# Mixer outputs normed with tokens in the rows, RWKV values centred on the way, and one of ten plans followed

## The chip, the cores and the metric

The kernel runs on one core of a Trainium2 chip. The metric is the device time of one execution in microseconds (us), the median of several runs. All data are float32. The core has a matrix engine (PE in the profile, with its weight loads shown as PEld), a vector engine (DVE), a scalar engine (ACT), GpSimd (POOL) and an engine that issues the DMAs (SP). Each follows its own instruction list in order and waits on semaphores for the others.

## The reference

Two layers of a streaming encoder over 1024 tokens of width 1024. Each layer is: RMS norm, one wide input projection, two mixers side by side, one output projection, RMS norm and residual add, and then a gated MLP of width 2816 with norm and residual. Layer 0 mixes with RWKV-7 (8 heads of 64) and a spatial gating unit; layer 1 with HGRN2 (8 heads of 64) and gated DeltaNet (4 heads of 128). The change touches only what happens to a mixer's output `y`, per token and head:

```python
# RWKV-7: layer norm over a head's 64 values, bonus, gate
mu_y = jnp.mean(y, axis=-1, keepdims=True)
var_y = jnp.mean(jnp.square(y - mu_y), axis=-1, keepdims=True)
y = ((y - mu_y) * lax.rsqrt(var_y + RWKV_LN_EPS) * ln_g + ln_b)
y = y + jnp.sum(rh * kh * r_k, axis=-1, keepdims=True) * vh
y = y * g
# HGRN2: RMS norm over a head's 64 values, then the gate
return merge_heads(rms_norm(o, norm_g)) * silu(gate)
# gated DeltaNet: RMS norm over a head's 128 values, then the gate
return merge_heads(rms_norm(o, norm_g)) * silu(z)
```

In RWKV-7 the state is linear in the values `v`, and so is `y`: if every `v` has its mean over the head's 64 channels taken away, so has `y`.

## The kernel before

**Two kinds of work share PE.** The projections and the MLP are dense matmuls (`dense`): weights come in pieces of 256 KB, ACT makes a rounded copy `wh` of each and DVE the remainder `wl`, and three matmuls `d<-h,wh`, `d<-l,wh`, `d<-h,wl` of 128 x 512 replace each float32 product (`mh`, `ml` in place of `h`, `l` in the second half of the MLP). The mixers are cut into units of 256 tokens and 128 channels: 16 RWKV units (`rwkv_unit`), 16 HGRN2 units (`hgrn_unit`) and 16 DeltaNet units (`gdn_unit`), each a chain of small float32 matmuls into PSUM banks called `m`, with short DVE, ACT and POOL steps between them. A unit has channels in the partitions and tokens in the columns; tokens come in 4 chunks of 64.

**A unit's tail before.** The products of all chunks are added up in one bank `py`, channels in the rows. RWKV copies it out (`yy`, on ACT), multiplies by the centring matrix `cen` on PE, squares on ACT (`sq`) and copies the centred values on DVE (`yc`). Then `rsqrt` sums the squares per head by a matmul with columns of ones (`m<-blk,sq`, or `m<-ones,sq` for DeltaNet), scales on DVE and takes the power -1/2 on POOL (`rt`), spreads the result over each head's 64 columns on ACT (`rw`; DeltaNet reads `rt` itself with a repeated column), and turns it on PE (`m<-ident,rw`, `m<-ident,rt`), so that two DVE steps can multiply by norm and weight. HGRN2 and DeltaNet do the same without the centring. RWKV ends with a gate matmul (`m<-L,gup`). Each result goes to DRAM by a DMA.

**The order is planned.** `Plan` records the whole program twice. The first pass only counts buffers; the second places every instruction by costs of its own on a clock of its own, always resuming the most urgent thread that can go (mixer units before the MLP). Where a unit reaches a `yield` with a list of tiles, it is not resumed until `MARGIN` (1.0 us on the plan's clock) after these are ready, and other threads fill PE until then. The order found is then fixed on each engine. At most 4 units are open at a time, and the input projection runs at most 1 unit group ahead.

Every instruction is issued from one helper line, L66, so tiles tell the profile's rows apart, not lines.

Of the kernel before, what the change touches and what calls it, by code (L numbers as in the profile page):

```python
# [23 lines left out]
C = 64  # L24
# [51 lines left out]
PACE = 0.8  # L76

MARGIN = 1.0
# [32 lines left out]
class Plan:  # L111
# [4 lines left out]
    def __init__(self, nc, past=None, tc=None):  # L116
        self.nc, self.past, self.tc = nc, past, tc
        names = ("tensor", "vector", "scalar", "gpsimd", "sync")
# [144 lines left out]
    def place(self, eng, method, outs, ins, scaled=False, func=None):  # L263
# [71 lines left out]
        t += c  # L335
        if eng == "tensor":
# [68 lines left out]
    def run(self, threads, queue, limit):  # L405


        units = 0
        self.live = live = list(threads)
        while live:  # L410
# [5 lines left out]
            if self.past:  # L416
                w = int(self.now // TICK)
                if self.work.get(w, 0.0) < PACE * 3060 * (self.now / TICK - w):
                    todo = [(t, u - 10 if x.dense else u, i, x) for t, u, i, x in todo]
# [12 lines left out]
            else:  # L432
                x.wake = max((self.ready.get(ap.tensor.name, (0.0, 0))[0] for ap in need), default=-MARGIN) + MARGIN


class Trunk:
    kp, kahead, over, smooth = 4, 2, 1, 1

    def __init__(self, ctx, tc, a, out, past=True):
        if past is True:  # L440
            past = forecast(a)
        self.h, self.l = ([[None] * 2 for _ in range(KT)] for _ in range(2))
        self.tc, self.nc, self.a, self.out = tc, Plan(tc.nc, past, tc), a, out
# [662 lines left out]


# [59 lines left out]
    def rwkv_unit(self, j, u, NC):  # L1167
# [215 lines left out]
        nc.vector.scalar_tensor_tensor(out=yy, in0=yy, scalar=col["ln_g"], in1=rs, op0=ALU.mult, op1=ALU.mult)  # L1383
        nc.vector.scalar_tensor_tensor(out=yy, in0=yy, scalar=col["ln_b"], in1=bon, op0=ALU.add, op1=ALU.add)
# [110 lines left out]
    def hgrn_unit(self, j, u, NC):  # L1495
# [83 lines left out]
        py = m()  # L1579
# [3 lines left out]
        for n in range(0 if S0 is not None else 1, NC):  # L1583
            for h in range(2):
# [3 lines left out]
        nc.vector.tensor_copy(yy, py[:, 0:W])  # L1588
        sq = t("sq", (P, W))
        nc.scalar.activation(sq, py[:, 0:W], AF.Square)  # L1590
        yield [sq]
        rs = yield from self.rsqrt(sq, 2, 1.0 / 64, 4 * EPS)
        nc.vector.scalar_tensor_tensor(out=yy, in0=yy, scalar=self.col["hhng"][:, j:j + 1], in1=rs, op0=ALU.mult, op1=ALU.mult)
        nc.vector.tensor_tensor(out=yy, in0=yy, in1=gate, op=ALU.mult)
# [104 lines left out]
    def gdn_unit(self, h, u, NC):  # L1699
# [115 lines left out]
        nc.vector.tensor_copy(yy, py[:, 0:W])  # L1815
        sq = t("sq", (P, W))
        nc.scalar.activation(sq, py[:, 0:W], AF.Square)
        yield [sq]
        rs = yield from self.rsqrt(sq, 1, 1.0 / P, EPS)
        nc.vector.scalar_tensor_tensor(out=yy, in0=yy, scalar=self.col["hgng"], in1=rs, op0=ALU.mult, op1=ALU.mult)  # L1820
        nc.vector.tensor_tensor(out=yy, in0=yy, in1=zz, op=ALU.mult)
# [50 lines left out]
    def run(self):  # L1872
# [7 lines left out]
        self.groups, self.workers, self.ahead = [5, 5, 4, 4, 4], 4, 1  # L1880
        self.urg = dict(unit=0, mix=-1, sgu=1, mixers=2, ffn=3, start=1, rows=2.5)
# [20 lines left out]
        self.nc.run(threads, self.units, self.workers)  # L1902
# [51 lines left out]
```

## Time and profile before

| | |
|---|---|
| median of 3 runs | 2949.36 us (2948.76 to 2951.91) |
| the profiled execution's own time | 2953.02 us |
| its span, first to last instruction | 2951.3 us |
| PE busy | 2836.7 us, 96% |
| DVE busy | 1843.5 us, 62% |
| ACT busy | 1258.8 us, 43% |
| POOL busy | 574.9 us, 19% |
| mean granted PE clock | 0.977 |

A matmul's span in these rows is longer than its share of PE, since the next one starts before it ends: 128 x 512 matmuls last some 0.4 us and start every 0.23 us. What one costs PE is read from the distance of starts in the timeline. A float32 matmul of the program shows as two records, a transpose as one, a dense matmul as one. In a timeline row `m<-blk,sq 128*128 128x2 f32 x4` the first product is the stationary operand's rows by columns, then the output's partitions by moving columns, then the number of records that stand one after another. Brackets at a row's end tell how long the engine had been idle, and what ended that.

### The profile page before, as it was taken

The numbers are of one execution on the slowest core, as the hardware profiler recorded it, in microseconds if no ns is written. First come the engines' busy times: TensorE is split into PE (matmuls) and PEld (weight loads), VectorE is DVE, ScalarE is ACT, GpSimd is POOL, SyncE is SP. The second block draws the span as 40 slices with busy tenths as digits, with TensorE's granted clock in tenths as the row PEclk, the third lists the DMA queues.
The fourth block names the chain that finished last, engine by engine and source line by source line (L and its number), as shares of the span: only waits on it lengthen the run. The fifth ranks groups of instructions, "written<-read, shape, count | busy, mean of one in ns | idle before, by whom it ended". The sixth has DMA issues, their size and how long they took to land. (4 is left out here: it accounts for less than half of the span.)

```text
span 2951.3 us, 46440 instructions
## 1 busy us (share of the span) xinstructions
PE 2836.7 (96%) x16608; PEld 2285.5 (77%) x16608; DVE 1843.5 (62%) x3747; ACT 1258.8 (43%) x2435; POOL 574.9 (19%) x1527
## 2 busy tenths in 40 slices
PE   7998999899999999999999999999999999999998
PEld 6776777778878877777778878777777888888886
DVE  4857686785574476666665676657666557554444
ACT  4445363454443355333334344543333335444333
POOL 1345233352000000323440000032343000000000
PEclk9998999899999999999999999999999999999999
DMA  6233244222443344545333444464642344343332
GB/s 178 66 88 83 73 141 129 56 71 80 128 141 91 99 141 86 90 72 68 77 77 114 127 121 125 104 97 60 83 82 62 93 133 134 107 127 88 108 96 93
DMA packets 560228, 294.13 MB, mean 100 GB/s; under 512 B 103293, under 2 KB 533198, under 8 KB 559998
## 3 DMA queue, kind: packets, MB, share of 16 engines
q1 hardware_dynamic: 559998, 291.17, 40.0%
q8 instruction: 131, 2.15, 0.3%
q14 instruction: 99, 0.81, 0.1%
HBM read 255.37 MB, written 35.71 MB: 99 GB/s over the span
## 5 line engine op out<-in xcount | busy, mean ns | idle before, releaser
L66 PE MATMUL d<-h,wh 128*128 128x512 f32 (+1 forms) x2544 | 1045.5, 411 | 0.0
L66 PE MATMUL d<-h,wl 128*128 128x512 f32 (+1 forms) x2544 | 1011.8, 398 | 4.9 <-DVE wl L66 4.9
L66 PE MATMUL d<-l,wh 128*128 128x512 f32 (+1 forms) x2544 | 1011.3, 398 | 0.0
L66 ACT CAST wh<-wr 128x512 fp32r<-128x512 f32 (+1 forms) x860 | 507.6, 594 | 700.7 <-PE d L66 555.2
L66 DVE TENSOR_TENSOR wl<-wr,wh 128x512 fp32r<-128x512 f32 (+1 forms) x860 | 560.4, 664 | 229.7 <-ACT wh L66 223.2
L66 PEld LDWEIGHTS d<-h,wl 128*128 128x128 f32 (+1 forms) x2544 | 482.6, 190 | 122.6 <-DVE wl L66 8.8
L66 PEld LDWEIGHTS d<-h,wh 128*128 128x128 f32 (+1 forms) x2544 | 483.6, 190 | 105.9 <-issue 2.2
L66 PEld LDWEIGHTS d<-l,wh 128*128 128x128 f32 (+1 forms) x2544 | 483.9, 190 | 98.3 <-issue 0.7
L66 POOL TENSOR_TENSOR rt<-rt,mhalf 128x4 f32<-128x4 f32 (+1 forms) x94 | 104.5, 1113 | 964.0 <-DVE rt L66 927.6
L66 PE MATMUL d<-mh,wh 128*128 128x512 f32 x704 | 283.9, 403 | 0.0
L66 PE MATMUL d<-mh,wl 128*128 128x512 f32 x704 | 279.3, 397 | 1.5 <-DVE wl L66 1.5
L66 PE MATMUL d<-ml,wh 128*128 128x512 f32 x704 | 279.1, 396 | 0.0
L66 DVE SCALAR_TENSOR_TENSOR t<-g,col,t 128x512 f32<-128x512 f32 x176 | 133.0, 755 | 168.0 <-ACT t L66 155.4
L66 POOL TENSOR_TENSOR itm<-iN,iPT 32x48 f32<-32x48 f32 (+15 forms) x480 | 160.6, 335 | 172.2 <-DMA iN<-ib 77.5
L66 POOL TENSOR_TENSOR iPT<-iPT,itm 32x48 f32<-32x48 f32 (+15 forms) x480 | 177.9, 371 | 36.2
L66 DVE TENSOR_TENSOR acc<-acc,d 128x512 f32<-128x512 f32 x128 | 88.0, 688 | 125.5 <-PE d L66 125.0
L66 PEld LDWEIGHTS d<-mh,wl 128*128 128x128 f32 x704 | 133.1, 189 | 34.2 <-DVE wl L66 3.2
L66 PEld LDWEIGHTS d<-mh,wh 128*128 128x128 f32 x704 | 133.4, 189 | 30.4 <-issue 0.2
L66 PEld LDWEIGHTS d<-ml,wh 128*128 128x128 f32 x704 | 133.3, 189 | 29.2 <-DVE ml L66 0.3
L66 ACT COPY g<-d 128x512 f32<-128x512 f32 x88 | 51.6, 587 | 149.7 <-PE d L66 149.3
L66 POOL COPY fhalo<-g 128x2 f32<-128x2 f32 x44 | 11.0, 249 | 473.3 <-ACT g L66 473.3
L66 DVE TENSOR_TENSOR sq<-sq 128x512 f32<-128x512 f32 x97 | 67.2, 693 | 23.7 <-ACT sq L66 17.7
(339 smaller groups left out, 3208.6 us busy)
## 6 DMA issues: line engine op xcount, KB each, us to landing
wr<-in_ffn_w_in SPq DMA_DIRECT2D x352, 256.0 KB
wr<-in_od_w_in SPq DMA_DIRECT2D x128, 256.0 KB
wr<-in_ffn_w_out SPq DMA_DIRECT2D x96, 256.0 KB
wr<-in_ev_w_in SPq DMA_DIRECT2D x84, 256.0 KB
xt<-xd SPq DMA_DIRECT2D x56, 256.0 KB
wr<-in_ffn_w_out SPq DMA_DIRECT2D x64, 192.0 KB
wr<-in_ev_w_out SPq DMA_DIRECT2D x32, 256.0 KB
yl<-yd SPq DMA_DIRECT2D x32, 256.0 KB
```

The source lines that it names most:

```text
L66: r = fn(*args, **kw)
```

## The change

**Tails.** In all three units the last products swap their operands, so that tokens stand in the rows of `py` and channels in the columns. A new function `normed_rows` squares on ACT straight from PSUM, sums per head with a DVE reduction, scales on DVE, takes the power on POOL, multiplies out of PSUM on DVE (`yt`), and only then transposes `yt` on PE. The sums by matmul, the spread `rw` and the turning of the norm go. HGRN2 now holds two banks, one per head, and squares and multiplies each by itself. **Centring.** RWKV's values `v` are transposed by a matmul with `cen` in place of the identity, so `y` comes out centred and the product with `cen` at the tail goes. **Plans.** `MARGIN` and other constants become fields of ten rules; each rule's plan is made, and the one whose end on the plan's clock is earliest is followed. For this program it is the second: everything as before, but a margin of 0.7 in place of 1.0.

```diff
-PACE = 0.8
-MARGIN = 1.0
+RULES = [dict(dict(pace=0.8, margin=1.0, workers=4, ahead=1, second=1), **r) for r in (
+    {}, dict(margin=0.7), dict(margin=0.85), dict(margin=1.3), dict(ahead=2), dict(second=-1), dict(workers=5),
+    dict(pace=0.9), dict(margin=0.7, ahead=2), dict(margin=0.85, workers=5))]
...
-                x.wake = max((self.ready.get(ap.tensor.name, (0.0, 0))[0] for ap in need), default=-MARGIN) + MARGIN
+                x.wake = max((self.ready.get(ap.tensor.name, (0.0, 0))[0] for ap in need), default=-margin) + margin
...
-            past = forecast(a)
+            past = forecast(a).digest()
+            rules = min(RULES, key=lambda r: forecast(a, past, r).end)
...
+    def normed_rows(self, pys, n, scale, eps):
+        nc, heads = self.nc, len(pys)
+        W = heads * pys[0].shape[1] * pys[0].shape[2]
+        def part(x, h):
+            return x.rearrange("p (i h c) -> p i h c", h=heads, c=pys[0].shape[2])[:, :, h]
+        sq = self.t("sq", (P, W))
+        for h, py in enumerate(pys):
+            nc.scalar.activation(part(sq, h), py, AF.Square)
+        r = self.t("rt", (P, 4))[:, 0:n]
+        nc.vector.tensor_reduce(out=r, in_=sq.rearrange("p (n c) -> p n c", n=n), op=ALU.add, axis=AX.X)
+        nc.vector.tensor_scalar(out=r, in0=r, scalar1=scale, scalar2=eps, op0=ALU.mult, op1=ALU.add)
+        nc.gpsimd.tensor_tensor(out=r, in0=r, in1=self.mhalf[:, 0:n], op=ALU.pow)
+        yt = self.t("yt", (P, W))
+        for h, py in enumerate(pys):
+            k, c = py.shape[1:]
+            rh = r[:, h::heads] if heads > 1 else r
+            nc.vector.tensor_tensor(out=part(yt, h), in0=py, in1=rh.unsqueeze(2).to_broadcast([P, k, c]), op=ALU.mult)
+        yield [yt]
+        ps = self.pst()
+        for i in range(W // P):
+            nc.tensor.transpose(ps[:, i * P:(i + 1) * P], yt[:, i * P:(i + 1) * P], self.ident)
+        return ps[:, 0:W]
...
@@ rwkv_unit
-            nc.tensor.transpose(ps[:, W + i * P:W + (i + 1) * P], v[:, i * P:(i + 1) * P], self.ident)
+            nc.tensor.matmul(ps[:, W + i * P:W + (i + 1) * P], v[:, i * P:(i + 1) * P], self.cen, start=True, stop=True)
...
-            for h in range(2):
-                s = slice(64 * h, 64 * h + 64)
-                nc.tensor.matmul(py[s, n * C:(n + 1) * C], Z[n][s, s], PR[s, n // 2, 1, 1 - n % 2], start=n == 0, stop=False)
+            nc.tensor.matmul(py[ts, n // 2 * P:n // 2 * P + P], PR[:, n // 2, 1, 1 - n % 2], Z[n], start=n < 2, stop=False)
...
-                nc.tensor.matmul(py[s, n * C:(n + 1) * C], ST[:, i, e, h], SC[h][:, i, e, C:P], start=False, stop=n == NC - 1)
+                nc.tensor.matmul(pv[ts, i, h], SC[h][:, i, e, C:P], ST[:, i, e, h], start=False, stop=n >= NC - 2 and h == 1)
+        ps = yield from self.normed_rows([py[:, 0:W].rearrange("p (n c) -> p n c", c=C)], 2 * I, 1.0 / 64, 64e-5)
         yy = t("yy", (P, W))
-        nc.scalar.copy(yy, py[:, 0:W])
-        yield [yy]
-        pc = m()
-        nc.tensor.matmul(pc[:, 0:W], self.cen, yy, start=True, stop=True)
-        sq = t("sq", (P, W))
-        nc.scalar.activation(sq, pc[:, 0:W], AF.Square)
-        yy = t("yc", (P, W))
-        nc.vector.tensor_copy(yy, pc[:, 0:W])
-        yield [sq]
-        rs = yield from self.rsqrt(sq, 2, 1.0 / 64, 64e-5)
-        nc.vector.scalar_tensor_tensor(out=yy, in0=yy, scalar=col["ln_g"], in1=rs, op0=ALU.mult, op1=ALU.mult)
-        nc.vector.scalar_tensor_tensor(out=yy, in0=yy, scalar=col["ln_b"], in1=bon, op0=ALU.add, op1=ALU.add)
+        nc.scalar.activation(yy, ps, AF.Identity, scale=col["ln_g"], bias=col["ln_b"])
+        nc.vector.tensor_tensor(out=yy, in0=yy, in1=bon, op=ALU.add)
@@ hgrn_unit
-                nc.tensor.matmul(py[64 * h:64 * h + 64, i * P:(i + 1) * P], VT[:, i, h], SC[h][:, i], start=i == 0, stop=False)
+                nc.tensor.matmul(pys[h][:, i], SC[h][:, i], VT[:, i, h], start=i == 0, stop=False)
...
-                nc.tensor.matmul(py[s, n * C:(n + 1) * C], R[s, :, n - 1] if n else S0[s], Q[s, n], start=False, stop=n == NC - 1)
+                nc.tensor.matmul(pys[h][ts, n // 2], Q[s, n], R[s, :, n - 1] if n else S0[s], start=False, stop=n >= NC - 2)
+        ps = yield from self.normed_rows(pys, 2 * I, 1.0 / 64, 4 * EPS)
         yy = t("yy", (P, W))
...
+        nc.vector.scalar_tensor_tensor(out=yy, in0=ps, scalar=self.col["hhng"][:, j:j + 1], in1=gate, op0=ALU.mult, op1=ALU.mult)
...
@@ gdn_unit
-            nc.tensor.matmul(py[:, i * P:(i + 1) * P], Vn[:, i], SC[:, i], start=True, stop=False)
-            for n in (2 * i, 2 * i + 1):
-                nc.tensor.matmul(py[:, n * C:(n + 1) * C], S[n], n3(qe)[:, n], start=False, stop=n % 2 == 1)
+            nc.tensor.matmul(py[:, i * P:(i + 1) * P], SC[:, i], Vn[:, i], start=i == 0, stop=False)
+        for n in range(NC):
+            i, ts = n // 2, slice(64 * (n % 2), 64 * (n % 2) + 64)
+            nc.tensor.matmul(py[ts, i * P:(i + 1) * P], n3(qe)[:, n], S[n], start=False, stop=n >= NC - 2)
+        ps = yield from self.normed_rows([py[:, 0:W].rearrange("p (n c) -> p n c", c=P)], I, 1.0 / P, EPS)
```

**The tail of the first RWKV unit, on PE, before.** From the last product into `py` (`SC,ST`) to the turning of the norm; `iQ`, `iU`, `X`, `iP` belong to another unit's inverse, `Z,WT` and `ST,QT` to another's chunk chain.

```order
L66 MATMUL m<-SC_1130,ST 64x64
L66 MATMUL m<-iQ,Ap 64x64 x8
L66 MATMUL m<-Z_2203,WT 128x128
L66 MATMUL m<-yy,cen 128x256
L66 MATMUL m<-iQ,iU 64x64 x8
L66 MATMUL m<-ST,QT 128x128
L66 MATMUL m<-blk,sq 128x2 x2
L66 MATMUL m<-X,iP 64x64 x8
L66 MATMUL m<-iP,PT 64x64 x8
L66 MATMUL m<-Z_2204,WT 128x128
L66 MATMUL m<-iR,Ap 64x64 x8
L66 MATMUL m<-ident,rw 128x128 x2
```

The tail comes back to PE three times, and its gate matmul is a fourth. The same tail in the changed program (the last product, now `ST,SC`, stands ten dense matmuls ahead of `Z,WT`; the last five of the ten are shown):

```order
L66 MATMUL d<-h,wl 128x512
L66 MATMUL d<-h,wh 128x512
L66 MATMUL d<-l,wh 128x512
L66 MATMUL d<-h,wl 128x512
L66 MATMUL d<-h,wh 128x512
L66 MATMUL m<-Z_2150,WT 128x128
L66 MATMUL m<-ident,yt 128x128 x2
L66 MATMUL d<-l,wh 128x512
L66 MATMUL m<-ST,QT 128x128
L66 MATMUL m<-L_647,gup 128x256
L66 MATMUL m<-L_491,wup 128x256 x2
```

It comes back once before the gate; ten dense matmuls and one small one stand between the products and that return.

**The tail of a DeltaNet unit, on PE, before.** `SC,Vn` and the products of the state (`gst`, `Sn`) with the queries (`eg`) go into `py`; twelve dense matmuls follow, then `m<-ones,sq 128x1 x2`, twelve more, then the turning of `rt`.

```order
L66 MATMUL m<-SC,Vn 128x128
L66 MATMUL m<-eg,gst 128x64
L66 MATMUL m<-eg,Sn 128x64
L66 MATMUL m<-SC,Vn 128x128
L66 MATMUL m<-eg,Sn 128x64 x2
L66 MATMUL d<-h,wh 128x512
```

And in the changed program, where eighteen dense matmuls follow, and then `m<-ident,yt 128x128 x2`:

```order
L66 MATMUL m<-Vn,Kd_12987 128x128
L66 MATMUL m<-Vn,SC 128x128 x2
L66 MATMUL m<-gst,eg 64x128
L66 MATMUL m<-Sn,eg 64x128 x3
L66 MATMUL d<-h,wh 128x512
```

The stationary operand is now the 64 tokens of a chunk, the moving one the 128 columns of the state. On PE the whole program goes from 64 `m<-blk,sq`, 16 `m<-yy,cen` and 156 `m<-ones,sq` to none, none and 124; 32 transposes of `v` become 32 matmuls with `cen`; 128 products `m<-PR,Z 64x64` become 64 `m<-Z,PR 64x128`. On ACT 48 spreads `rw` become 16. The dense matmuls are 9744 in both.

More of the change, by code (lines that the diff above doesn't have):

```diff
@@ L111, with __init__ @@
 class Plan:
-    def __init__(self, nc, past=None, tc=None):
+    def __init__(self, nc, past=None, tc=None, rules=RULES[0]):
         self.nc, self.past, self.tc = nc, past, tc
+        self.rules, self.end = rules, 0.0
         names = ("tensor", "vector", "scalar", "gpsimd", "sync")
@@ L335, in place @@
         t += c
+        self.end = max(self.end, t)
         if eng == "tensor":
@@ L405, in run @@
     def run(self, threads, queue, limit):
-        units = 0
+        units, margin = 0, self.rules["margin"]
         self.live = live = list(threads)
@@ L417, in run @@
                 w = int(self.now // TICK)
-                if self.work.get(w, 0.0) < PACE * 3060 * (self.now / TICK - w):
+                if self.work.get(w, 0.0) < self.rules["pace"] * 3060 * (self.now / TICK - w):
                     todo = [(t, u - 10 if x.dense else u, i, x) for t, u, i, x in todo]
@@ L1577, in hgrn_unit @@
         yield [R, SC[1]]
-        py = m()
+        pys = [x[:, 0:I * C].rearrange("p (i c) -> p i c", i=I) for x in (m(), m())]
         for i in range(I):
             for h in range(2):
-                nc.tensor.matmul(py[64 * h:64 * h + 64, i * P:(i + 1) * P], VT[:, i, h], SC[h][:, i], start=i == 0, stop=False)
+                nc.tensor.matmul(pys[h][:, i], SC[h][:, i], VT[:, i, h], start=i == 0, stop=False)
         for n in range(0 if S0 is not None else 1, NC):
+            ts = slice(64 * (n % 2), 64 * (n % 2) + 64)
             for h in range(2):
                 s = slice(64 * h, 64 * h + 64)
-                nc.tensor.matmul(py[s, n * C:(n + 1) * C], R[s, :, n - 1] if n else S0[s], Q[s, n], start=False, stop=n == NC - 1)
+                nc.tensor.matmul(pys[h][ts, n // 2], Q[s, n], R[s, :, n - 1] if n else S0[s], start=False, stop=n >= NC - 2)
+        ps = yield from self.normed_rows(pys, 2 * I, 1.0 / 64, 4 * EPS)
         yy = t("yy", (P, W))
[L1588 to L1594, printed above, removed]
+        nc.vector.scalar_tensor_tensor(out=yy, in0=ps, scalar=self.col["hhng"][:, j:j + 1], in1=gate, op0=ALU.mult, op1=ALU.mult)
         nc.sync.dma_start(self.yd[hf][j * P:(j + 1) * P, at:at + W], yy)
@@ L1810, in gdn_unit @@
         for i in range(I):
-            nc.tensor.matmul(py[:, i * P:(i + 1) * P], Vn[:, i], SC[:, i], start=True, stop=False)
-            for n in (2 * i, 2 * i + 1):
-                nc.tensor.matmul(py[:, n * C:(n + 1) * C], S[n], n3(qe)[:, n], start=False, stop=n % 2 == 1)
-        yy = t("yy", (P, W))
[L1815 to L1821, printed above, removed]
+            nc.tensor.matmul(py[:, i * P:(i + 1) * P], SC[:, i], Vn[:, i], start=i == 0, stop=False)
[3 more added lines that the diff above has]
+        ps = yield from self.normed_rows([py[:, 0:W].rearrange("p (n c) -> p n c", c=P)], I, 1.0 / P, EPS)
+        yy = t("yy", (P, W))
+        nc.vector.scalar_tensor_tensor(out=yy, in0=ps, scalar=self.col["hgng"], in1=zz, op0=ALU.mult, op1=ALU.mult)
         nc.sync.dma_start(self.yd[hf][A_W + h * P:A_W + (h + 1) * P, at:at + W], yy)
@@ L1879, in run @@
                 self.st[(n, j, 0)] = None
-        self.groups, self.workers, self.ahead = [5, 5, 4, 4, 4], 4, 1
-        self.urg = dict(unit=0, mix=-1, sgu=1, mixers=2, ffn=3, start=1, rows=2.5)
+        self.groups, self.ahead = [5, 5, 4, 4, 4], self.rules["ahead"]
+        self.urg = dict(unit=0, mix=-1, sgu=1, mixers=2, ffn=3, start=self.rules["second"], rows=2.5)
         threads = []
@@ L1901, in run @@
         add("mixers", 0, 0, self.mixers(), None)
-        self.nc.run(threads, self.units, self.workers)
+        self.nc.run(threads, self.units, self.rules["workers"])
         for c in self.nc.order.values():
@@ L1912, with forecast @@
     pass
-def forecast(a):
+def forecast(a, past=None, rules=RULES[0]):
     import concourse.bacc as bacc
@@ L1923, in forecast @@
         with tile.TileContext(nc) as tc, ExitStack() as ctx:
-            trunk = Trunk(ctx, tc, b, out[0], past=None)
+            trunk = Trunk(ctx, tc, b, out[0], past, rules)
             trunk.run()
@@ L1927, in forecast @@
     except Traced:
-        return trunk.nc.digest()
+        return trunk.nc
 _INS = ["x", "norm_mix_pre", "norm_mix_post", "norm_ffn_pre", "norm_ffn_post", "ev_w_in", "ev_w_out", "rwkv_mu",
```

9 lines of the change are left out of this document (6 added, 3 removed).

## Prediction

> **What bounds the kernel now.** I read the page first (engines' shares), then the table of stretches, then the timeline of PE around the tails.
>
> ```profile
> span 2951.3 us, 46440 instructions
> PE 2836.7 (96%) x16608; PEld 2285.5 (77%) x16608; DVE 1843.5 (62%) x3747; ACT 1258.8 (43%) x2435; POOL 574.9 (19%) x1527
> ```
>
> PE is busy for 2836.7 of 2951.3 us, so 114.6 us idle; no other engine is above 62%. The table of stretches (columns: us, PE busy with its records, PEld, DVE, ACT, POOL, granted PE clock, DMA share, GB/s) says where that idle time lies and what a pure dense stretch costs:
>
> ```profile
> 0.00:738.00 738.00, 678.27 (x5546) 542.61 (x5547) 495.96 (x1280) 340.16 (x752) 263.63 (x678) 0.96 0.36 97
> 738.00:2951.30 2213.30, 2158.47 (x11063) 1742.86 (x11061) 1347.49 (x2468) 918.61 (x1683) 311.30 (x849) 0.98 0.42 101
> 2656.00:2730.00 74.00, 74.00 (x321) 59.92 (x320) 34.25 (x55) 29.82 (x54) 2.21 (x5) 1.00 0.31 88
> ```
>
> In the last row PE never rests, the clock is full, and a matmul takes 74.00 / 321 = 0.2305 us. In the first 738 us, layer 0, PE idles for 59.7 us and the clock of 0.96 takes another 0.04 x 738 = 30 us; in the 2213 us behind it, 54.8 us idle and 0.02 x 2213 = 44 us. How many matmuls are dense, from the page's costliest groups (three groups of each of these two counts):
>
> ```profile
> L66 PE MATMUL d<-h,wh 128*128 128x512 f32 (+1 forms) x2544 | 1045.5, 411 | 0.0
> L66 PE MATMUL d<-mh,wh 128*128 128x512 f32 x704 | 283.9, 403 | 0.0
> ```
>
> 3 x (2544 + 704) = 9744 dense records at 0.2305 us are 2246 us. The other 6864 records have 2836.7 - 2246 = 591 us, 0.086 us each, with the slow clock and the changes between kinds in it. So time here is mostly the length of PE's list: what shortens the list shortens the run, unless PE waits more.
>
> **The change, part by part: PE's list.** A price is the distance from a row's start to the next row's. RWKV, one tail and its neighbours:
>
> ```profile
> 214.29 0.61 PE L66 MATMUL m<-blk,sq 128*128 128x2 f32 x4
> 214.76 0.47 PE L66 MATMUL m<-ST,QT 128*128 128x128 f32 x2
> 215.16 0.68 PE L66 MATMUL m<-PR,Z 64*64 64x64 f32 x16
> 215.77 0.69 PE L66 MATMUL m<-SC,ST 128*64 128x64 f32 x16
> ...
> 216.87 0.60 PE L66 MATMUL m<-ident,rw 128*128 128x128 f32 x4
> 217.30 0.63 PE L66 MATMUL m<-yy,cen 128*128 128x256 f32 x2
> 217.77 0.38 PE L66 MATMUL m<-ST,QT 128*128 128x128 f32 x2
> ```
>
> The norm's sums cost 0.47 us, the centring 0.47, the 16 records of `PR,Z` 0.61, and two transposes half of 0.43, 0.22. Products of the new shapes stand in DeltaNet units:
>
> ```profile
> 1303.78 0.66 PE L66 MATMUL m<-KQ,cs 128*64 128x128 f32 x8
> 1304.37 0.66 PE L66 MATMUL m<-ident,cs 128*128 128x128 f32 x4
> ...
> 1324.52 0.39 PE L66 MATMUL m<-SC,Vn 128*128 128x128 f32 x2
> 1324.74 0.33 PE L66 MATMUL m<-eg,gst 128*128 128x64 f32 x2
> 1324.91 0.39 PE L66 MATMUL m<-eg,Sn 128*128 128x64 f32 x2
> 1325.13 0.44 PE L66 MATMUL m<-SC,Vn 128*128 128x128 f32 x2
> 1325.41 0.56 PE L66 MATMUL m<-eg,Sn 128*128 128x64 f32 x4
> ```
>
> The new `Z,PR` is 8 records of the shape of `KQ,cs`, 0.59 us. `v` through `cen` is 4 records of the shape of `SC,Vn` (0.22 or 0.28 a pair), so 0.44 to 0.56 instead of 0.22; I take +0.25. `SC,ST` keeps its shape when swapped, and two transposes of `yt` replace two of `rw`. RWKV unit: -0.47 - 0.47 - 0.61 + 0.59 + 0.25 = -0.71 us, times 16 units -11.4 us (bounds -11.8 and -9.9, from the two ends for `cen`).
>
> DeltaNet loses `ones,sq`, here two tails in one row of 8:
>
> ```profile
> 1350.66 1.05 PE L66 MATMUL m<-ones,sq 128*128 128x1 f32 x8
> 1351.64 0.66 PE L66 MATMUL m<-SC,KV 128*64 128x128 f32 x8
> ```
>
> 0.98 / 2 = 0.49 us. The queries' products were 0.17 + 0.22 a pair, 0.78 for all 8, and become 8 records of the `KQ,cs` shape, 0.59: -0.19. `SC,Vn` keeps its shape, `rt` and `yt` are both two transposes. Unit: -0.68, times 16 = -10.9 us (if the swap brings nothing: -7.8).
>
> HGRN2:
>
> ```profile
> 1269.50 0.66 PE L66 MATMUL m<-SC,KV 128*64 128x128 f32 x8
> 1270.09 0.33 PE L66 MATMUL m<-z,S 64*64 64x64 f32 x4
> 1270.26 0.88 PE L66 MATMUL m<-z,R 64*64 64x64 f32 x12
> 1270.97 0.40 PE L66 MATMUL m<-iQ,iU 64*64 64x64 f32 x8
> ```
>
> It loses `blk,sq`, -0.47. `SC,KV` goes from 0.59 us to 8 records of the `eg` shape (0.17 or 0.22 a pair: 0.68 to 0.88; I take 0.78 as above), +0.19. The state products now keep `Q` and stream `R`, whose columns lie 16 bytes apart. I take 0. Below it, they become as quick as `z,S` (0.17 / 4 = 0.043 against 0.71 / 12 = 0.059): -0.19. Above it, as slow as the 8 records of `KQ,cs` (0.074): +0.18. The step costs something as a weight load already:
>
> ```profile
> L66 PEld LDWEIGHTS m<-z,R 64*64 64x64 f32 x192 | 12.7, 209 | 2.2 <-DVE R L66 1.4 <-issue 0.5 <-DVE S L66 0.2
> L66 PEld LDWEIGHTS m<-z,S 64*64 64x64 f32 x48 | 2.3, 131 | 2.1 <-issue 2.1
> ```
>
> 209 against 131 ns, nearest to "no change of sides". Unit: -0.28, times 16 = -4.5 us (bounds -9.1 and 0). The Trainium skill, page "SBUF — State Buffer", section "Door 1: The DMA port swizzle", says that SBUF is read in lines of 16 bytes, that two hits on a line are needed for full rate, and that a float32 stride of 4 or more pays. By that rule the streamed `R` pays on every element, and the HGRN2 term would be near its bound of 0; the two weight-load rows agree that the stride costs, and no row here streams such an operand.
>
> Together -26.8 us (bounds -31.8 and -17.7). The record counts say the same: 320 fewer at 0.086 us are 27.5 us.
>
> **Other engines.** In each unit DVE trades a copy out of PSUM and a multiply for a reduction and a multiply, and RWKV saves a multiply more; ACT loses 32 spreads `rw` and 16 copies `yy`, and gains 16 of `yy` behind the transpose. At 62% and 43% these engines follow PE, whose dense matmuls hide the difference; I count 0. Without that cover it would count at the last unit of each half alone, four times, where the output projection waits. What counts is the path back to PE, `sq`, sum, scale, power, multiply:
>
> ```profile
> L66 ACT ACTIVATE sq<-m x48: 362/384/406, 194.1 to 2359.4; 128x256 f32<-128x256 f32 x48
> L66 DVE TENSOR_REDUCE var<-sq x8: 666/685/689, 77.5 to 381.6; 128x8 f32<-128x512 f32 x8
> L66 POOL TENSOR_TENSOR rt<-rt,mhalf 128x4 f32<-128x4 f32 x78 | 91.6, 1175 | 842.6 <-DVE rt L66 811.0 <-ACT wh L66 25.4 <-PE m L66 4.1
> L66 DVE TENSOR_TENSOR Kd<-m,GE 128x256 f32<-128x256 f32 x32 | 11.9, 415 | 0.0
> ```
>
> 0.38 + half of 0.685 + some 0.15 + 1.18 + 0.42 = 2.5 us, and with five hand-overs and DVE's and ACT's queues 3 to 4. In the order of the first RWKV tail only ten dense matmuls and one small one cover it, 10 x 0.2305 + 0.2 = 2.5 us, so PE stands before `yt` with all its list behind it; the DeltaNet tail has eighteen, 4.1 us, which just covers. So a new wait, on `yt`: I take +3 us in all 48 tails (bounds 0 and 10, a full 1 us in ten of them). It replaces waits on `yy` and partly `rw`:
>
> ```profile
> PE m L66 <- DVE Vn L66: 4.4, 2, 2.3
> PE m L66 <- ACT yy L66: 1.8, 2, 1.2
> PE m L66 <- ACT rw L66: 1.5, 3, 0.8
> ```
>
> (us in total, times, longest): -2 us.
>
> **The plan.** Following a margin of 0.7 moves every thread's return 0.3 us closer to its producers. In layer 0 that shortens chains where PE has too little to do; afterwards PE is full, and the same 0.3 us only brings PE nearer to a producer that is late. I take 0 between these, with bounds of -45 and +52 us, which are the rivals below.
>
> Sum: -26.8 + 3 - 2 = -26 us. The profiled execution took 2953.0 us (span 2951.3 and 1.7 around it), 3.7 us above the median of 2949.4. So 2927 for a profiled run and **2923 us** for the median. Less than 0.2% (5.9 us) can't be told from no change.
>
> **Rivals.** *(a) Stalls shrink too.* The first 738 us hold 60 + 30 us of idle and slow clock. Tails return to PE two times fewer and each return comes 0.3 us sooner. If half of that loss goes, 45 us more: 2878. For: PE is short of work only there. Against: the order there shows tails covered by no more than 2.5 us.
>
> *(b) New waits eat the gain.* Counted from the code, units come back to PE by a `yield` some 22 (RWKV), 17 (DeltaNet) and 6 (HGRN2) times, 16 x 45 = 720. If one in eight is now late by the 0.3 us taken away, 90 x 0.3 = 27 us: 2950, no change.
>
> *(c) Slower.* The same mechanism at one in four: 180 x 0.3 = 54 us, 2977; it decides from about 110 late returns on (33 us). For: the plan picks by its own costs, and a plan that cuts the margin looks good to costs that are too low. Against: today, of 64 returns on `Vn` two waited, of 48 on `rw` three, so one in twenty. Each late return can cost more than its wait, since the clock falls:
>
> ```profile
> 223.10 0.85 PE L66 MATMUL m<-L,wup 32*128 32x256 f32 x2 [0.38 <-DVE yc L66]
> ...
> 224.47 0.63 PE L66 MATMUL d<-l,wh 128*128 128x512 f32 x1
> 224.90 0.63 PE L66 MATMUL d<-h,wl 128*128 128x512 f32 x1
> ```
>
> Here dense matmuls follow at 0.43 us, half speed, behind a wait of 0.38 us. The Trainium skill, page "TensorE: Matmul & The Clock Gate", section "What's actually happening", has the clock halved after an idle window of about 3.4 us; this row's idle time is far shorter, so here the measurement decides, and short waits are not free.
>
> *(d) Only part is relieved*: the swaps cost their upper bounds, the `yt` waits theirs: -17.7 + 10 - 2 = -10, 2940.
>
> **Numbers.** Forecast 2923 with 0.50, (a) 0.17, (d) 0.12, (b) 0.12, (c) 0.09. The forecast's own range is 2905 to 2938. The range 2878 to 2955 leaves out half of (a), all of (c) and a quarter of (b), 0.2 together. Faster: the forecast, (a), most of (d) and a quarter of (b), 0.80; within 0.2%: half of (b) and the rest of (d), 0.08; slower: (c) and a quarter of (b), 0.12.
>
> **What would show it.** PE's busy time falls to about 2810 us with 16288 records; `yt` transposes of two records take 0.22 us, `Z,PR` 0.59 for 8, `R,z` 0.71 for 12. PE's idle time stays near 115 us and the clock near 0.977; `PE m <- DVE yt` is a few us. Wrong, if PE's idle time moves by more than 30 us either way: then the plan, not the list, made the result. (c) would show as more small waits on `Vn`, `ST`, `Z` and `yt` behind 738 us.

## The result, and the profile after

The changed kernel takes 2971.35 us (median of 6 runs, 2966.76 to 2979.66) against 2948.45 us before (6 runs, 2945.84 to 2951.91) in the same comparison: ratio 1.008, 95% interval 1.007 to 1.009. It is slower by 23 us; forecast was 26 us faster. The time lies outside the range, on its slow side.

The page of the changed kernel, its span and the engines' shares; below it PE by stretches (us, PE busy with its records, PEld, DVE, ACT, POOL, granted PE clock, DMA share, GB/s):

```profile
span 2970.0 us, 45766 instructions
PE 2811.7 (95%) x16288; PEld 2258.1 (76%) x16288; DVE 1829.7 (62%) x3751; ACT 1246.7 (42%) x2409; POOL 561.0 (19%) x1527
```

```profile
0.00:738.00 738.00, 663.74 (x5348) 528.34 (x5349) 492.16 (x1280) 336.51 (x734) 255.86 (x678) 0.95 0.36 96
738.00:1200.00 462.00, 457.76 (x1996) 369.51 (x1995) 280.58 (x453) 205.70 (x355) 14.01 (x53) 0.99 0.43 114
1200.00:2320.00 1120.00, 1051.15 (x6051) 840.41 (x6051) 704.02 (x1463) 440.41 (x867) 274.92 (x745) 0.96 0.46 88
```

The third of these stretches in the kernel before:

```profile
1200.00:2320.00 1120.00, 1083.50 (x6315) 871.36 (x6314) 720.17 (x1473) 451.59 (x884) 278.71 (x746) 0.98 0.44 91
```

PE's list did what was forecast: 16288 records, busy 2811.7 us (forecast 2810), 25.0 less than before. But PE's idle time rose from 114.6 to 158.3 us, by 43.7. Of that, 14.5 us are in the first 738 us (59.7 to 74.3) and 32.4 between 1200 and 2320 us (36.5 to 68.9), where HGRN2 and DeltaNet units run. Between 738 and 1200 us, where no unit runs and POOL does next to nothing (14 us), PE idles for 4 us. The granted clock went from 0.977 to 0.970. The prediction had named PE's idle time moving by more than 30 us as the sign that the plan, not the list, made the result; that sign is here.

What PE waits for, in the changed kernel (waited for, us in total, times, longest):

```profile
PE m L66 <- DVE K L66: 34.5, 8, 8.0
PE m L66 <- DVE yt L66: 24.2, 10, 10.8
PE m L66 <- DMA iR<-ir: 14.4, 7, 6.7
...
PE m L66 <- DVE Z L66: 9.8, 7, 4.2
PE m L66 <- DVE ST L66: 7.7, 7, 2.6
```

and the largest of the kernel before:

```profile
PE m L66 <- DVE K L66: 15.2, 5, 6.3
```

These are not many small waits on everything, but a few long ones. `K` is HGRN2's, `yt` the new tail's. The waits of DVE in the changed kernel say what is behind both:

```profile
DVE yt L66 <- POOL rt L66: 44.6, 36, 7.4
DVE K L66 <- POOL itm L66: 31.9, 6, 8.2
DVE cum L66 <- POOL itm L66: 12.7, 2, 6.9
```

Both are POOL. `rt` is the tail's power. `itm` and `iPT` are the steps of a 16-row elimination that starts each unit's triangular inverse (`inverse_base`, 30 steps a unit, on POOL). In the kernel before, the wait for the power stood on ACT, and DVE's largest behind `itm` was small; first ACT, then DVE:

```profile
ACT rw L66 <- POOL rt L66: 51.5, 29, 3.7
```

```profile
DVE cum L66 <- POOL itm L66: 8.2, 2, 4.4
DVE dd L66 <- POOL itm L66: 7.3, 1, 7.3
```

The longest wait for `yt`, from the changed kernel's timeline (start, length, engine, instruction, idle time before it and what ended that):

```profile
515.21 0.41 DVE L66 TENSOR_REDUCE rt<-sq 128x4 f32<-128x256 f32 x1
515.65 0.22 DVE L66 TENSOR_SCALAR rt<-rt 128x4 f32<-128x4 f32 x1
515.78 0.68 DVE L66 TENSOR_TENSOR sq<-sq 128x512 f32<-128x512 f32 x1
515.91 0.73 POOL L66 TENSOR_TENSOR iPT<-iPT,itm 32x63 f32<-32x63 f32 x1
...
518.74 0.30 POOL L66 TENSOR_TENSOR iPT<-iPT,itm 32x60 f32<-32x60 f32 x1
...
522.62 0.27 POOL L66 TENSOR_TENSOR iPT<-iPT,itm 32x48 f32<-32x48 f32 x1
522.86 1.00 POOL L66 TENSOR_TENSOR rt<-rt,mhalf 128x4 f32<-128x4 f32 x1
523.89 0.42 DVE L66 TENSOR_TENSOR yt<-m,rt 128x256 f32<-128x256 f32 x1 [7.43 <-POOL rt L66]
524.46 0.66 PE L66 MATMUL m<-ident,yt 128*128 128x128 f32 x2 [10.79 <-DVE yt L66]
525.15 0.63 ACT L66 ACTIVATE sq<-row 128x512 f32<-128x512 f32 x1 [9.92 <-DVE row L66]
```

The power's input is ready at 515.9. But POOL takes its instructions in order, and 21 elimination steps, 7 us in all, stand before it. So the power comes 7 us late, DVE stands at `yt` with all its queue behind it, and PE and ACT stand still too.

### The profile page after: what moved, and what is told of

The parts are those of the page before. It is cut to its first block, busy times and chain, and to the rows that moved or that the text cites. A ratio compares the mean times of both kernels' runs of the same rounds, so it can differ in the third digit from the quotient of the medians.

```text
span 2970.0 us, 45766 instructions
## 1 busy us (share of the span) xinstructions
PE 2811.7 (95%) x16288; PEld 2258.1 (76%) x16288; DVE 1829.7 (62%) x3751; ACT 1246.7 (42%) x2409; POOL 561.0 (19%) x1527
## 4 chain that ended last, share of the span: by engine, by line
PE 37%; issue 7%; POOL 3%; DMA 2%; DVE 1%; ACT 0%; SPq 0%; POOLq 0%; DVEq 0%; ACTq 0%
PE d L66 33%; PE m L66 4%; POOL iPT L66 2%; POOL itm L66 1%; DMA wr<-in_od_w_in 1%; DMA iR<-ir 1%; DMA ib<-Ap 0%; DVE co L66 0%; DVE xo L66 0%; SPq L66 0%; POOL rt L66 0%; DVE row L66 0%; DMA iN<-ib 0%; DVE wl L66 0%; DVE t L66 0%
## 5 line engine op out<-in xcount | busy, mean ns | idle before, releaser
L66 POOL TENSOR_TENSOR itm<-iN,iPT 16x39 f32<-16x39 f32 (+15 forms) x480 | 161.0, 336 | 228.3 <-DMA iN<-ib 121.4
L66 POOL TENSOR_TENSOR iPT<-iPT,itm 32x39 f32<-32x39 f32 (+15 forms) x480 | 174.1, 363 | 36.3
L66 DVE TENSOR_TENSOR t<-t,d 128x512 f32<-128x512 f32 x70 | 48.1, 687 | 63.0 <-PE d L66 61.7
```

The costliest lines, as they stand in the source:

```text
L66: r = fn(*args, **kw)
```

## The experiments

### Other rules: is it the shorter margin?

Theories: **M**, the margin of 0.7 makes returns late (rival (c)); **T**, the new tails' wait for `yt`; **P**, any new plan strays from the chip by an amount of its own.

```diff
+RULES = [dict(dict(pace=0.8, margin=1.0, workers=4, ahead=1, second=1))]
```

> The change with its first rule alone: new tails and centring, margin 1.0 as before. Theory M (the shorter margin makes PE meet late producers): PE's idle time falls back from 158 to about 115 us, PE stays busy for about 2812 us, and the median is about 2925 us (2915 to 2935). Theory T (the tails' own new wait on yt is the loss): it stays at 2960 to 2975 with some 20 us of waits on yt. Theory P (any new plan differs from the chip by its own amount, the shorter margin being one of many): anywhere between 2920 and 2975, and not in the order of the margins.

2982.91 us, ratio 1.0108 (1.0092 to 1.0125).

```diff
+RULES = [dict(dict(pace=0.8, margin=1.0, workers=4, ahead=1, second=1), margin=1.3)]
```

> The change with a margin of 1.3 alone. Theory M: fewer short waits than at 1.0, 2915 to 2930 us. Theory T: as the change, 2960 to 2975. Theory P: anywhere between 2920 and 2975, waits of several us on K, yt and the inverse's loads as in the change.

2945.59 us, 0.9982 (0.9973 to 0.9991). PE waits for `yt` for 5.0 us here.

```diff
+RULES = [dict(dict(pace=0.8, margin=1.0, workers=4, ahead=1, second=1), ahead=2)]
```

> The change with margin 1.0 and the input projection up to 2 unit groups ahead, another of the ten rules. Theory M: about 2925 us as with margin 1.0. Theory T: 2960 to 2975. Theory P: anywhere between 2910 and 2975.

2963.96 us, 1.0046 (1.0031 to 1.0061). The wait for `yt` is 4.0 us.

The kernel before, with only its margin changed:

```diff
-MARGIN = 1.0
+MARGIN = 0.7
```

> The kernel before with a margin of 0.7: old tails. Theory M: PE's idle time grows from 115 to about 155 us as it did with the change, and the median is 2980 to 2995 us. Theory T: 2945 to 2955. Theory P: anywhere between 2930 and 2995.

2979.48 us, 1.0092 (1.0075 to 1.0109).

With the margin at 1.0 the change is slower still, so M alone is not it. With one rule or another it moves by 37 us, and the old kernel by 29 for a margin alone. So the verdict on the change hangs on the rule: at 0.7 the two kernels can't be told apart (1.007 to 1.009 and 1.0075 to 1.0109), at 1.0 the changed one is 32 us slower. T is a part at most: the time does not follow the wait for `yt`. P comes nearest, but 2983 us lies above its range too, and it names no cause.

### The plan's buffers

`Plan` hands out buffers on its own clock. The program's tiles are given real ones by the tile library, by another rule. Where these differ, a DVE or ACT step can get a buffer that POOL's elimination still reads, a wait that the plan doesn't know. The edit gives each tile of the three large SBUF kinds the numbered buffer that the plan chose; the order on every engine is the same, instruction by instruction.

```diff
-                self.ready[name] = self.free[tag].pop(0), ""
+                at, self.slot[name] = self.free[tag].pop(0)
+                self.ready[name] = at, ""
...
-        return self.nc.tile(self.tp.tile(list(shape), dt, tag=tag, name=name, bufs=n), tag, n)
+        real, bufs = self.seat(tag, n)
+        return self.nc.tile(self.tp.tile(list(shape), dt, tag=real, name=name, bufs=bufs), tag, n)
+    def seat(self, tag, n):
...
+        return "slot" + tag + str(nc.free[tag][0][1]), 1
```

> The changed kernel, its plan and its order on every engine unchanged; only the SBUF buffers differ: a tile of the three large kinds now gets the very buffer that the plan's clock gave it, where before the buffer that the program gets is not the plan's. Theory S (DVE and ACT steps wait because the chip's buffer is one that POOL's inverse still reads, a wait that the plan doesn't know): DVE's idle time behind POOL's itm, 51 us in the changed kernel (K 31.9, cum 12.7, SC 4.8 and smaller), falls below 10, PE's wait for K from 34.5 to below 10, and the time to 2925 to 2948. Theory Q (POOL is late by its own queue: inverse steps slower than the plan's, powers behind them): 2963 to 2978, the waits for yt stay near 24 us. Theory D (a new plan differs from the chip in many small ways, none of which stands out): K's wait moves elsewhere, 2960 to 2975.

2946.06 us, 0.9991 (0.9982 to 1.0001): 25 us less. The change with its plan's buffers, DVE's only wait for `itm` in the table, and PE's two largest waits:

```profile
DVE R L66 <- POOL itm L66: 1.3, 1, 1.3
```

```profile
PE m L66 <- DVE yt L66: 23.9, 11, 9.3
PE m L66 <- DVE K L66: 15.2, 4, 6.2
```

So S holds for 25 us: 51.5 us of DVE's idle time behind `itm` became 1.3, and PE's wait for `K` fell by 19 (to 15, not below 10 as expected). The wait for `yt` did not move.

> As the run before, and PSUM's banks m and d also as the plan gave them. S: as the run before, at most 8 us less, 2918 to 2948. Q and D: 2960 to 2978.

2941.57 us, 0.9979 (0.9970 to 0.9988). The intervals of this run and the one before it overlap: what PSUM's banks bring, 4 us by the medians, can't be told from nothing.

> The kernel before, order unchanged, with the plan's buffers. DVE's idle time behind POOL's itm is 21 us there. S: it gains less than the changed kernel does, 5 to 20 us: 2930 to 2945; the gap between the two kernels with the plan's buffers is then about what the prediction said, the changed one lower by 0 to 25 us. Q and D: 2944 to 2954, and the changed kernel stays 15 to 25 us slower.

2929.95 us, 0.9945 (0.9929 to 0.9962). The old kernel gains 19 us by the same edit, and is faster than both kernels of this case. S had the changed kernel ahead by 0 to 25 us once both have their plan's buffers; it is 16 us behind. So the buffers cost the two kernels nearly the same; the difference is 7 of the 49 us between forecast and result.

The same edit with margins of 1.0 and 1.3:

> The change with margin 1.0 for every wait (2983 us with the program's own buffers), here with the buffers of its plan; order unchanged. Theory S: DVE's idle time behind itm, 41 us there, goes, and with it as many us, 2938 to 2952. Theory D: under 12 us less, 2970 to 2983.

2949.11 us, 1.0001 (0.9992 to 1.0010): 34 us less.

> The change with margin 1.3 (2946 us with the program's own buffers), here with the plan's buffers in SBUF and PSUM; order unchanged. Theory S: DVE's idle time behind itm, 21 us there, goes: 2916 to 2930, faster than either kernel. Theory D: 2938 to 2948.

2938.01 us, 0.9964 (0.9952 to 0.9976): 8 us less, where 16 to 30 were expected. In this kernel PE now waits 23.7 us for `iR` and 12.1 for `yt`.

> The kernel before with margin 1.3 and the plan's buffers in SBUF and PSUM: the same rule and the same buffers as the run before this one, without the change's tails. If a wider margin serves every wait alike: 2915 to 2930, at most 10 us from the changed one. If it serves the new tails above all, whose wait for yt is 24 us at 0.7 and 5 at 1.3: 2930 to 2950. If the shorter list comes through once rule and buffers are equal, the changed one is 15 to 30 us faster than this.

2933.92 us, 0.9947 (0.9931 to 0.9962). The last two can't be told apart (their intervals overlap): under one rule and with both plans' buffers the shorter list shows no gain. In the old kernel DVE still idles for 15.7 us behind `itm` there, 11.4 of them in one wait. With margin 1.0 the change is even slower than the old kernel (2949 against 2930).

| kernel, margin | DVE idle behind `itm` | time | with the plan's buffers |
|---|---|---|---|
| before, 1.0 | 21 us | 2948 | 2930 |
| changed, 0.7 | 51 us | 2971 | 2946 |
| changed, 1.0 | 41 us | 2983 | 2949 |
| changed, 1.3 | 21 us | 2946 | 2938 (PSUM too) |

The second column is the sum of the rows "DVE ... <- POOL itm" in the table of waits. The wide spread between these three margins, 2946 to 2983, was mostly buffers: with the plan's buffers it is 2938 to 2949.

### POOL's elimination steps

```diff
+            nc.mute = 1 < s < 15
             nc.gpsimd.tensor_tensor(out=tm[0:n, 0:s, s:], in0=N[0:n, 0:s, s:s + 1].to_broadcast(sh),
                                     in1=Q[:, s:s + 1, s:].to_broadcast(sh), op=ALU.mult)
             nc.gpsimd.tensor_tensor(out=Q[:, 0:s, s:], in0=Q[:, 0:s, s:], in1=tm[0:n, 0:s, s:], op=ALU.subtract)
+            nc.mute = False
```

(A muted instruction is placed by the plan, but not issued.)

> The changed kernel, plan and order unchanged, but 13 of the 15 elimination steps of each 16-row inverse on POOL are left out (so the inverse is not the reference's); the plan still counts them. POOL's inverse work falls by some four fifths of 335 us. S: what waits for POOL's reads of the inverse's buffers no longer waits: 2920 to 2948, much as with the plan's buffers. Q: the waits for yt (24 us), for iR (14 us) and K go: 2915 to 2940, clearly below the run with the plan's buffers. D: 2955 to 2970.

2883.62 us, 0.9786 (0.9772 to 0.9801): 31 us below the lowest bound of the three ranges.

> The kernel before, plan and order unchanged, with the same 13 of 15 elimination steps of each inverse on POOL left out (so the inverse is not the reference's). In the changed kernel that brought 88 us (2971 to 2884). Theory Q, now in the form that POOL's inverse is what ate the gain of the shorter list: with POOL nearly idle both kernels take what their lists take, so the kernel before ends about 26 us above the changed one, 2902 to 2918. Theory E (POOL holds up both kernels alike, and the changed one has lost its gain in other waits): it also gains 80 to 95 us, 2853 to 2870, and stays ahead of the changed one by 10 to 30.

2887.62 us, 0.9793 (0.9779 to 0.9807). PE and POOL in the two, the changed kernel first:

```profile
PE 2780.4 (97%) x16288; PEld 2238.5 (78%) x16288; DVE 1818.2 (63%) x3751; ACT 1246.1 (43%) x2409; POOL 270.3 (9%) x695
```

```profile
PE 2804.3 (97%) x16608; PEld 2260.3 (78%) x16608; DVE 1824.2 (63%) x3747; ACT 1259.2 (44%) x2435; POOL 279.4 (10%) x695
```

The steps hold the changed kernel up for 88 us and the old one for 61, although POOL is busy for only 19% of the time. The 27 us between are more than the whole 23 us by which the change is slower: without POOL's steps the two are alike. Neither expectation of the second run was met: it lies between them. The gain didn't return either: PE's list is still 23.9 us shorter, and PE idles as much more (spans of 2881.1 and 2881.8 us, so 100.7 against 77.5 us idle).

These 88 and 61 us are not idle time alone. In the changed kernel PE's busy time fell by 31.3 us with the same 16288 records (2811.7 to 2780.4), at a granted clock of 0.984 in place of 0.970; in the old one by 32.4, at 0.989 in place of 0.977. Nor do these two runs separate POOL's queue from the buffers that its steps hold (25 and 19 us above) or from what the steps and DVE cost each other.

### The wait for the power

```diff
             nc.vector.tensor_tensor(out=part(yt, h), in0=py, in1=rh.unsqueeze(2).to_broadcast([P, k, c]), op=ALU.mult,
+                                    swap=self.ones[:, 0:k].unsqueeze(2).to_broadcast([P, k, c]))
```

(`swap` is what the instruction reads in place of `in1`; the plan still places it by `in1`.)

> The changed kernel with its plan's buffers (2946 us), order unchanged on every engine; the multiply yt takes a column of ones in place of the norm, which is still computed (so the outputs are not normed). All instructions stay; only DVE's wait at yt for POOL's power goes. Theory H (before, ACT waited for the power, at rw, 51.5 us in 29 waits; now DVE does, at yt, 45.1 us in 37 waits, and in DVE's queue all short steps of the other units stand behind it): DVE's idle time behind rt goes to about 1, PE's idle time from 141 to 112 to 122 us, the time to 2915 to 2930. Theory L (DVE has time to spare at 62%, the wait at yt is hidden): 2938 to 2948.

2936.73 us, 0.9959 (0.9944 to 0.9974): 9 us less than with the plan's buffers alone, where H had 16 to 31 and L 8 at most. PE's waits:

```profile
PE m L69 <- DVE Z L69: 17.4, 7, 8.8
...
PE m L69 <- DVE yt L69: 10.8, 5, 5.2
```

The wait for `yt` falls by 13 us, but `Z` rises from 10.6 to 17.4: DVE's `Z` waits for a memset of POOL's that stands in the same queue. Getting past the late power, DVE runs into the next thing that POOL is late with.

The multiply moved to ACT, in the same plan:

```diff
-            nc.vector.tensor_tensor(out=part(yt, h), in0=py, in1=rh.unsqueeze(2).to_broadcast([P, k, c]), op=ALU.mult)
+            nc.vector.tensor_tensor(out=part(yt, h), in0=py, in1=rh.unsqueeze(2).to_broadcast([P, k, c]), op=ALU.mult,
+                                    emit=lambda: [nc.scalar.eng.activation(part(yt, h)[:, i], py[:, i], AF.Identity, scale=rh[:, i:i + 1])
+                                                  for i in range(k)])
```

(The plan places the multiply on DVE as before; `emit` is what is issued in its place, on ACT.)

> The changed kernel with its plan's buffers (2946 us), plan unchanged; the multiply yt is taken off DVE and done on ACT, one instruction per group of 64 or 128 columns with the norm as the scale, at the same place in time. So ACT waits for POOL's power again, as before the change. H: 2912 to 2932, PE's wait for wl and short DVE steps falls. L, and a rival in which ACT, with some 160 more instructions of 0.2 to 0.25 us, now holds up wh and the dense matmuls: 2940 to 2956.

2942.77 us, 0.9984 (0.9971 to 0.9996). Not told apart from DVE's version (0.9982 to 1.0001). PE waits for `yt` as long as before (26.7 us): it is POOL that is late, whoever waits.

With another margin, and planned on ACT:

```diff
-            nc.vector.tensor_tensor(out=part(yt, h), in0=py, in1=rh.unsqueeze(2).to_broadcast([P, k, c]), op=ALU.mult)
+            for i in range(k):
+                nc.scalar.activation(part(yt, h)[:, i], py[:, i], AF.Identity, scale=rh[:, i:i + 1])
```

> The change with margin 1.3, the plan's buffers in SBUF and PSUM (2938 us), and yt on ACT, planned so. H: 2908 to 2926, faster than the kernel before by over 0.8%. L: 2932 to 2945.

2933.94 us, 0.9955 (0.9941 to 0.9970), against 0.9952 to 0.9976 with `yt` on DVE: no clear gain, and H missed again.

> The changed kernel, plan and order unchanged, both with POOL's elimination steps left out (2884 us by themselves) and with yt not waiting for the norm (outputs neither normed nor from the full inverse). To be held against the kernel before with the same steps left out, 2888 us. If what is left of the change without POOL's two ways of holding it up is the shorter list, at the rate at which dead work on PE's list counted (11 of 24.6 us): 26 x 0.45 = 12 us below the kernel before, 2872 to 2879. If the waits just move on: 2880 to 2886.

2882.93 us, 0.9779 (0.9763 to 0.9796), as without the second edit (2883.62). That is what was expected if the waits just move on; the 12 us of gain by the rate of the dead products, 2872 to 2879, did not come (it is 5 us below the old kernel's 2888, and the intervals overlap). With the elimination steps alone left out, DVE's waits at `yt` were these:

```profile
DVE yt L68 <- POOL rt L68: 28.5, 37, 1.1
```

So there are still 37 of them, but none is longer than 1.1 us, and taking them away changes nothing.

### Is PE's list the bound?

```diff
             nc.tensor.transpose(ps[:, i * P:(i + 1) * P], yt[:, i * P:(i + 1) * P], self.ident)
+        for i in range(1 if heads > 1 else 3):
+            r = nc.tensor.eng.matmul(ps[:, 256:384], self.ones, self.ident, start=True, stop=True)
...
```

(What is left out fixes the products' place in PE's order.)

> The changed kernel with its plan's buffers (2946 us), order unchanged; behind each tail's transposes of yt PE does dead products of constants, three in an RWKV or DeltaNet unit, one in an HGRN2 unit, 112 in all at about 0.22 us, 24.6 us: as much as the change took off PE's list. If PE's list sets the time where the units run, as the prediction had it: 2964 to 2974. Theory C (there PE waits for the units' chains, and idle time takes the products up): 2944 to 2956.

2957.22 us, 1.0026 (1.0010 to 1.0042), 11 us more, just above theory C's range; the other begins at 2964. The kernel with its plan's buffers alone, then with the dead products:

```profile
PE 2800.6 (95%) x16288; PEld 2248.4 (76%) x16288; DVE 1831.0 (62%) x3751; ACT 1245.7 (42%) x2409; POOL 567.5 (19%) x1527
PE 2825.7 (96%) x16512; PEld 2277.9 (77%) x16512; DVE 1831.3 (62%) x3751; ACT 1246.6 (42%) x2409; POOL 564.6 (19%) x1527
```

PE is busy for 25.1 us more (2800.6 to 2825.7). The median rises by 11.2 us, and by the intervals of the two runs that could be some 5 to 16; the two profiled executions lie 15.7 apart (spans of 2941.2 and 2956.9), with 9.4 us less idle time. So idle time takes up a part of the list, and an estimate from these figures is that a microsecond of PE's list in a tail is worth 0.4 to 0.6 us in this kernel.

### A plan that counts what POOL costs

The plan's prices against the durations in the trace of the changed kernel with its plan's buffers: `iPT<-iPT,itm` 0.265 against 0.368 us, `itm<-iN,iPT` 0.272 against 0.341, the power 0.93 against 1.07, DVE's scans of 256 elements 0.34 against 0.70. DVE's larger element-wise steps are 8 to 15% dearer than planned and were left alone.

```diff
-                return 0.154 + n * 0.0019 if n < 100 else 0.09 + n * 0.00222
+                return 1.37 * (0.154 + n * 0.0019) if n < 100 else 0.09 + n * 0.00222
...
-                    return 0.28 + n * 0.167
+                    return 0.40 + n * 0.167
...
+        if eng == "vector" and "scan" in method:
+            return 0.12 + n * 0.0023
```

> The change with the plan's buffers in SBUF and PSUM, yt on ACT, and a plan that counts what the traces show: POOL's elimination steps 1.37 times dearer, its power 0.12 us dearer, DVE's scans 0.65 us instead of 0.34. One of the ten rules is picked as before; it is margin 0.7 with two unit groups ahead. If the plan's low prices for POOL are what made it late (theory Q): 2900 to 2925, the fastest of all. If not: 2928 to 2948.

2873.09 us, 0.9741 (0.9727 to 0.9756): 98 us less than the change as it was made, 76 less than the kernel before, with nothing left out. Its page, two stretches, and PE's largest waits:

```profile
span 2867.9 us, 45803 instructions
PE 2788.2 (97%) x16288; PEld 2242.2 (78%) x16288; DVE 1825.5 (64%) x3703; ACT 1280.9 (45%) x2575; POOL 570.7 (20%) x1527
```

```profile
0.00:738.00 738.00, 694.76 (x5503) 556.85 (x5504) 511.63 (x1299) 363.26 (x828) 253.26 (x684) 0.97 0.38 103
1200.00:2320.00 1120.00, 1099.13 (x6374) 880.83 (x6374) 732.41 (x1475) 488.22 (x1009) 271.25 (x705) 0.99 0.47 96
```

```profile
PE m L66 <- DMA iR<-ir: 9.6, 5, 5.3
PE d L66 <- DVE wl L66: 9.4, 10, 2.1
```

POOL has as much to do as ever (570.7 us), but the instructions that need it now stand where it can deliver, and `K` and `yt` are gone from the head of the table. PE's idle time is 79.7 us, half of the 158.3, and with the same 16288 records it is busy for 23.5 us less, at a granted clock of 0.985 in place of 0.970. Theory Q had the sign, and the run came out 27 us below its range. The plan's clock fits better too: there the change as it was made ends at 2883 us, 88 before the chip, and this one at 2889, 16 after it.

What made it so fast is not separated. The run differs from the one with `yt` on ACT and margin 1.3 (2934 us) in POOL's prices, in the price of DVE's scans and in the rule that was picked. That rule is not the one that the expectation names. By the kernel's own forecast the ten rules end between 2889 and 2935 us: the first of these is a margin of 0.85 with one group ahead, and 0.7 with two groups ahead ends at 2912. DVE's 3703 instructions stand in the trace in the order of the plan with 0.85. No other run has this margin. With their plans' buffers, margins of 0.7 and 1.0 took 2946 and 2949 us, so that one between them brings most of the 61 us is unlikely, but neither the prices nor the rule were tried alone.

## Why the prediction was wrong

**PE's list: right.** -26.8 us forecast, -25.0 measured, at the forecast count of records (PE's busy time also holds the lower clock). Its terms in the changed kernel's timeline:

```profile
211.77 0.66 PE L66 MATMUL m<-Z,PR 128*64 128x128 f32 x8
212.26 0.69 PE L66 MATMUL m<-ST,SC 128*64 128x64 f32 x16
...
216.69 0.61 PE L66 MATMUL m<-cen,z 128*128 128x128 f32 x4
217.14 0.38 PE L66 MATMUL m<-ident,yt 128*128 128x128 f32 x2
217.28 0.47 PE L66 MATMUL d<-h,wl 128*128 128x512 f32 x1
...
1338.95 1.10 PE L66 MATMUL m<-KV,SC 128*128 128x64 f32 x8
1339.99 0.66 PE L66 MATMUL m<-R,z 64*64 64x64 f32 x12
1340.57 0.49 PE L66 MATMUL d<-h,wh 128*128 128x512 f32 x1
```

`Z,PR` takes 0.49 us (0.59 forecast), `v` through `cen` 0.45 (0.47). In HGRN2 both sub-terms missed, in opposite directions: `KV,SC` takes 1.04 us (0.78 taken, 0.88 the bound), and `R,z` 0.58 (0.71 taken). The row read for `ones,sq` was a dear one: 0.98 us for 8 records, where the median of the 30 such rows before is 0.81, so that term was some 1.4 us too large.

**"What shortens the list shortens the run, unless PE waits more": half wrong.** PE's 96% was taken for a bound. But PE waits more: 43.7 us. In the tails a microsecond on its list was worth an estimated 0.4 to 0.6 (the dead products), so that the 25 us would be worth 10 to 15, and 10 to 15 of the 49 us that were missed would be explained. That rate did not hold where it was tried: without POOL's steps and without the wait at `yt` it gave 12 us of gain, and 5 were measured.

**"The plan. ... I take 0": this step failed.** The new plan wasn't neutral. It leans on POOL, whose steps it prices 20 to 28% too low, and on buffers that are not the ones the program gets. POOL's steps hold up the changed kernel for 27 us more than the old one (88 against 61). That is the largest part of the miss. The plan's end on its own clock, by which it was picked, was earlier than the old plan's (2883 against 2897 us); the chip's was later. With the measured prices, the plan's buffers and `yt` on ACT, the same ten rules led to 2873 us. That the low prices are why the new plan leans on POOL more than the old one did is argued, not shown: both plans have them.

**"`yt`: +3 us (bounds 0 and 10)": failed, 24.2.** The path was added up at 2.5 us, 3 to 4 with queues, of DVE and ACT. POOL's queue, where the power stands behind other units' elimination steps, was not in it: up to 7 us. **"Other engines. ... I count 0"** failed with it. Before, ACT's `rw` took the wait for the power, 51.5 us in 29 times; the change hands it to DVE, 44.6 us in 36, on which the units' short steps queue. Not having DVE wait is worth 9 us. It isn't the core of the miss, since without POOL's steps it is worth nothing (2883 with and without).

**The removed waits on `yy` and `rw`**, -2 us, were too small to matter.

**Rival (c)** had the sign and nearly the number (2977), which is luck in part: its mechanism, 0.3 us less for every return, is not what the changed kernel shows, since a margin of 1.0 made it slower, not faster. In the old kernel the shorter margin did cost 29 us, but PE's largest wait there is again `K`, 36.8 us in 8 times, and not the many small waits that (c) named. One sentence of it was right, in a rival with a chance of 0.09: a plan "looks good to costs that are too low".

Of the 49 us, then, 27 go with POOL's steps; the buffers and the wait for the power overlap with them. The other 22, the gain of the list that doesn't appear even without POOL's steps, stay open: PE then idles for 23 us more than in the old kernel, and no run settles why. Whether the old kernel, planned by the measured prices, would be as fast as 2873 us was not tried, so what the new tails are worth under a good plan stays open too.

**The clock and the streamed `R`.** PE's mean granted clock was 0.96 in 1200 to 2320 us, where the waits are, and 0.99 in 738 to 1200; that agrees with the quoted row, but no run here separates how long a wait must be. The Trainium skill, page "SBUF — State Buffer", section "Door 1: The DMA port swizzle", would have had the streamed `R`, with columns 16 bytes apart, pay. The trace disagrees for this operand: 0.58 us for 12 records where the same products took 0.71 with `R` as the weights, and the 15 such rows before have a median of 0.81.

## What to carry to other kernels

An engine that is busy for 19% of the time can hold up one that is busy for 96%: if it takes its work in order, what counts is what stands ahead of an instruction in its queue, not its share. Where a change hands a wait from one engine to another, read how long the first one stood there and who queues behind the second. And where a plan sets the order, hold its prices and its buffers against the trace before counting on what it picks: here measured prices, the plan's buffers, another margin and `yt` on ACT together were worth 98 us, four times what the shorter list was to bring.

## What the chip showed that was not expected

- POOL's steps depend on what DVE does. In the timeline above the step at 515.91 takes 0.73 us, while DVE's `sq<-sq` adds two SBUF tiles until 516.46; the step at 518.74, nearly as large, takes 0.30 with DVE idle. Over the whole trace the 224 elimination steps that start during a DVE step with two SBUF inputs have a median of 0.57 us, the 392 beside an idle DVE one of 0.27. The Trainium skill, page "SBUF — State Buffer", section "SBUF: two separate sides", has DVE and GpSimd share a pair of ports that one holds for a whole instruction while the other waits. These rows agree; the plan of this kernel charges for it too, but too little.
- A DVE scan of 128 x 256 elements takes 0.70 us, an element-wise multiply of that size 0.42.
- Swapping the operands of `SC,KV` made it slower, 1.04 us for 8 records in place of 0.59, although fewer columns are streamed (64 in place of 128). The stationary operand has 128 columns in place of 64, and its load went from 137 to 192 ns. Before, then after (shortest, median and longest, ns):

```profile
L66 PEld LDWEIGHTS m<-SC,KV x128: 132/137/231, 1253.2 to 2294.8; 128*64 128x64 f32 x128
```

```profile
L66 PEld LDWEIGHTS m<-KV,SC x128: 186/192/194, 1247.6 to 2309.6; 128*128 128x128 f32 x128
```
